# One decoder layer on one core: the small float32 products of two attention heads, and of two state-space groups, made in one visit of TensorE

## The chip, the core and the metric

The kernel runs on one NeuronCore of a Trainium2 chip. The metric is the device time of one execution in microseconds (us), the median of several runs.

## The reference, cut to what matters

The layer normalizes `x` (256 tokens, 2048 channels), multiplies it by one wide input matrix and gives the columns to three branches, whose results are gated, merged, multiplied by an output matrix, added to `x` and normalized again. Two of the branches are touched here.

```python
# stick-breaking attention, 8 heads of 128
logits = einsum('bqhd,bkhd->bhqk', q_blk, k) * scale
log_beta = log_sigmoid(logits)
log_keep = where(earlier, log_beta - logits, 0.0)
later = cumsum(log_keep, axis=3, reverse=True) - log_keep
weights = where(earlier, exp(log_beta + later), 0.0)
out = einsum('bhqk,bkhd->bqhd', weights, v)

# state-space branch, 8 groups of 4 heads, one chunk of 256 tokens
cb = einsum('bclgn,bcsgn->bcgls', cm, bm)
y_diag = einsum('bcgls,bgecls,bcsgep->bclgep', cb, decay_in, xs)
```

The third branch is an attention into 256 memory tokens.

## The kernel before, in words

**The stream of wide products.** Nearly all work is a sequence of matrix products over weights that are read from memory once. A product is cut into chunks. `gemm` (L248) takes chunks of two blocks of 128 input channels by 512 columns, `gemm_cols` (L210) chunks of four such blocks by 256 columns. Each chunk's weights arrive by a DMA of the SP queue in `raw` (four buffers). `split` (L141) then makes two parts of them: ScalarE (ACT) copies `raw` to `wh`, rounded to the fp32r format (L145), and VectorE (DVE) writes the remainder `raw - wh` to `wl` (L149). TensorE (PE) multiplies with both parts in fp32r (L268 to L270 in `gemm`, L228 and L232 in `gemm_cols`). `wh` and `wl` have three buffers each (the pool `stage`, L53), so the `wh` of a chunk can be written only when PE is done with the chunk three places before it. Within a chunk of `gemm_cols` PE first makes two products with `wh` (L228) and then two with `wl` (L232), four times over.

**The order of the other work.** After each chunk the program calls `pump` (L184). It first runs what was put off to this point by `defer` (L171), then one step of one generator. The generators wait in two lanes, and the chunks serve the lanes in turn, so that a generator moves by one step every second chunk. A step issues some instructions and ends at a `yield`. Every engine executes its own instructions in the order in which the program issues them. So the place of an instruction on ACT, between which two chunks' `wh`, is set by the number of `yield`s ahead of it, and nothing is looked up at run time.

**The attention heads.** `sb_head` (L684) is such a generator, and even heads stand in lane 0 and odd ones in lane 1. One head takes these steps: the logits `slg` (L688, L689), two matrix products in plain float32; scale and mask on DVE (L692, L695); `Abs`, `Exp` and `Ln` on ACT, which are the softplus (L698 to L700); a sum and a difference (L702 on DVE, L703 on GpSimd); the split of it (L707); the running sums `scu` in fp32r (L712, L714); a difference (L717); `Exp` on ACT (L719); the value products `spo` in plain float32 (L722, L724); the gating and a split (L728, L731). The heads run while the wide products for the state-space gate `zT` (L746) and then for the convolution channels (L801, `gemm_cols`) stream. The results `oS` are first used by the product with `w_branch_sb` (L984).

**The convolution stage.** Its results are folded (L245 on ACT, L246 on DVE) and go through four taps on DVE (L759 and three of L762), for one half of the columns and, two chunks later, for the other. From the fifth of its eight groups on, the loop at L799 also puts off three `Silu` each, over `zT` and then over the convolution channels (L806, executed in `silu`, L202).

**Function tables.** ACT evaluates `Silu` with another function table than `Exp` and `Ln`. Where the next function is not in the table that is loaded, an `ACT_TABLE_LOAD` stands in ACT's queue ahead of it, put there when the program is compiled. In the state-space part and for the memory heads the program loads a table that holds both `Exp` and `Ln` by hand (L661, L818). In `sb_head` it doesn't.

**The state-space groups.** `ssd_group` (L827) begins with two DMAs on the SP queue and the product `cb` of B and C (L839, L840), in plain float32. `cbs` (L855) is ACT's copy of it. The products `y` (L888) of two neighbouring groups are already made in one step. The eight groups stand in the same lanes behind the heads.

All the small products write to one of four buffers of accumulator memory (`bank`, L87), in turn.

## Time and profile before

| | |
|---|---|
| median of 3 runs | 1207.49 us (1207.31 to 1207.68) |
| the profiled execution's own time | 1207.59 us |
| its span, first instruction to last | 1205.8 us |
| PE busy | 1197.1 us, 99% of the span |
| DVE busy | 802.4 us, 67% |
| ACT busy | 633.8 us, 53% |
| GpSimd (POOL) busy | 49.2 us, 4% |
| granted TensorE clock, mean over the span | 0.998 of full speed |

A row of the profile names the source line, the engine, the operation and the tiles as output<-inputs. A duration runs from an instruction's start on its engine to its end. On PE and ACT the next instruction can start before that end, so that the step from one start to the next is what an instruction costs in a row of them. A float32 product appears as two passes of the same shape, each with a weight load (PEld). "[1.73 <-PE acc L228]" behind a row says that the engine sat idle for 1.73 us before it, until that instruction of PE ended.

### The profile page before, as it was taken

The page shows a single profiled execution, that of the slowest core. Times are in us where ns is not written, and L with a number is a line of the kernel's source. Part 1 is how long each engine was busy: PE and PEld are TensorE (multiplying, and loading weights), DVE is VectorE, ACT ScalarE, POOL GpSimd, SP SyncE. Part 2 cuts the span into 40 slices and gives each one's busy share as a digit, 9 for nine tenths or more (in the row PEclk, how much of TensorE's full clock was granted, in tenths as well). Part 3 has the DMA queues.
Part 4 walks back from the last instruction along what each step waited for, and adds up shares of the span by engine and source line. Part 5 has one row for each costly group of instructions (what it writes and reads, how often), then busy time and mean ns, then how long its engine had stood idle before and what let it go on. Part 6 is the DMA issues. An engine that isn't in the chain of part 4 may idle for free.

```text
span 1205.8 us, 15624 instructions
## 1 busy us (share of the span) xinstructions
PE 1197.1 (99%) x5814; PEld 1005.9 (83%) x5814; DVE 802.4 (67%) x1051; ACT 633.8 (53%) x834; POOL 49.2 (4%) x48
## 2 busy tenths in 40 slices
PE   9999999999999999999999999999999999999997
PEld 8888888888888888888888888888888888888886
DVE  6777664545655555888887858677677655565662
ACT  6665443354355444545655756484757534444551
POOL 0000000000000000010100000000000010110011
PEclk9999999999999999999999999999999999999999
DMA  9677787877765778666668676667766677778952
GB/s 342 224 221 228 226 238 232 250 235 216 211 202 173 208 232 226 185 182 175 175 185 260 209 224 217 210 206 220 226 177 203 206 220 219 228 224 278 301 198 88
DMA packets 168652, 261.52 MB, mean 217 GB/s; under 512 B 11840, under 2 KB 67840, under 8 KB 168448
## 3 DMA queue, kind: packets, MB, share of 16 engines
q1 hardware_dynamic: 134592, 227.94, 63.1%
q10 hardware_dynamic: 33984, 32.59, 8.2%
q8 instruction: 45, 0.74, 0.3%
q14 instruction: 31, 0.25, 0.1%
HBM read 245.78 MB, written 14.71 MB: 216 GB/s over the span
## 4 chain that ended last, share of the span: by engine, by line
PE 98%; issue 1%; DVE 0%; ACT 0%; POOL 0%; POOLq 0%; DVEq 0%; ACTq 0%
PE acc L268 25%; PE acc L270 25%; PE acc L269 25%; PE acc L228 10%; PE acc L232 5%; PE acc L473 4%; PE y L888 1%; PE warm L110 0%; PE dtp L531 0%; PE acc L1089 0%; PE acc L1087 0%; PE acc L1088 0%; PE spo L722 0%; PE slg L688 0%; PE cb L839 0%
## 5 line engine op out<-in xcount | busy, mean ns | idle before, releaser
L149 DVE TENSOR_TENSOR wl<-raw,wh 128x1024 fp32r<-128x1024 f32 (+1 forms) x410 | 504.9, 1233 | 302.6 <-ACT wh L145 296.9
L145 ACT ACTIVATE wh<-raw 128x1024 fp32r<-128x1024 f32 (+1 forms) x410 | 431.9, 1054 | 439.0 <-PE acc L270 339.0
L268 PE MATMUL acc<-wh,hT 128*128 128x512 f32 x896 | 350.9, 392 | 0.0
L270 PE MATMUL acc<-wh,hT 128*128 128x512 f32 x896 | 348.8, 389 | 0.0
L269 PE MATMUL acc<-wl,hT 128*128 128x512 f32 x896 | 348.8, 389 | 0.0
L270 PEld LDWEIGHTS acc<-wh,hT 128*128 128x128 f32 x896 | 168.2, 188 | 35.5
L268 PEld LDWEIGHTS acc<-wh,hT 128*128 128x128 f32 x896 | 168.3, 188 | 34.0 <-issue 0.3
L269 PEld LDWEIGHTS acc<-wl,hT 128*128 128x128 f32 x896 | 168.3, 188 | 33.6
L228 PE MATMUL acc<-hT,wh 128*128 128x512 f32 x512 | 161.5, 397 | 0.0
L232 PEld LDWEIGHTS acc<-hT,wl 128*128 128x128 f32 x512 | 96.2, 188 | 22.7
L232 PE MATMUL acc<-hT,wl 128*128 128x256 f32 x512 | 100.7, 278 | 0.0
L228 PEld LDWEIGHTS acc<-hT,wh 128*128 128x128 f32 x512 | 78.0, 189 | 0.1
L268 PE MATMUL acc<-wh,oD 128*128 128x512 f32 x128 | 49.8, 389 | 0.0
L269 PE MATMUL acc<-wl,oD 128*128 128x512 f32 x128 | 49.8, 389 | 0.0
L270 PE MATMUL acc<-wh,oD 128*128 128x512 f32 x128 | 49.8, 389 | 0.0
L762 DVE SCALAR_TENSOR_TENSOR cT<-cu,wcols,cT 128x255 f32<-128x255 f32 (+2 forms) x96 | 46.4, 483 | 3.4
L969 POOL TENSOR_TENSOR merged<-merged,sig 128x512 f32<-128x512 f32 x16 | 25.8, 1636 | 512.3 <-DVE sig L968 512.3
L268 PE MATMUL acc<-wh,mT 128*128 128x512 f32 x96 | 37.3, 389 | 0.0
L269 PE MATMUL acc<-wl,mT 128*128 128x512 f32 x96 | 37.3, 389 | 0.0
L270 PE MATMUL acc<-wh,mT 128*128 128x512 f32 x96 | 37.3, 389 | 0.0
L473 PE MATMUL acc<-wh,memT 128*128 128x512 f32 x128 | 32.4, 394 | 0.0
L473 PEld LDWEIGHTS acc<-wh,memT 128*128 128x128 f32 x128 | 24.2, 190 | 4.9
(250 smaller groups left out, 1258.6 us busy)
## 6 DMA issues: line engine op xcount, KB each, us to landing
raw<-in_w_in_dram SPq DMA_DIRECT2D x288, 512.0 KB, 4.3
raw<-in_w_branch_ssd_dram SPq DMA_DIRECT2D x32, 512.0 KB, 4.7
raw<-in_w_mem_kv_dram SPq DMA_DIRECT2D x31, 512.0 KB, 5.3
scratch<-blocks ACTq DMA_DIRECT2D x24, 512.0 KB, 4.5
raw<-in_w_out_dram SPq DMA_DIRECT2D x24, 512.0 KB, 6.2
turned<-scratch ACTq DMA_DIRECT2D x64, 128.0 KB, 4.5
raw<-in_w_branch_mem_dram SPq DMA_DIRECT2D x16, 512.0 KB, 4.8
raw<-in_w_branch_sb_dram SPq DMA_DIRECT2D x16, 512.0 KB, 5.0
```

Source lines behind the costliest of these rows:

```text
L145: nc.scalar.activation(hi, src, AF.Copy, **({} if scale is None else {"scale": scale}))
L149: nc.vector.tensor_tensor(lo, src, h32, ALU.subtract)
L228: nc.tensor.matmul(halves[b], wh[:, kt - k0, b * P:(b + 1) * P], lhs.both(kt), start=first, stop=False, skip_group_check=True)
L232: nc.tensor.matmul(halves[b][:, 1], wl[:, kt - k0, b * P:(b + 1) * P], lhs.at(kt)[0], start=False, stop=last, skip_group_check=True)
L268: nc.tensor.matmul(a, lh[:, tt], wh[:, j], start=first, stop=False)
L269: nc.tensor.matmul(a, lh[:, tt], wl[:, j], start=False, stop=False)
L270: nc.tensor.matmul(a, ll[:, tt], wh[:, j], start=False, stop=last)
L473: nc.tensor.matmul(acc[g][:, t], a[:, t * P:(t + 1) * P], w[:, g], start=(k == 0 and i in (0, 3)), stop=(k == NKT - 1 and i > 3))
L762: nc.vector.scalar_tensor_tensor(a[:, s:T], u[:, 0:T - s], convw[:, 3 - s, i:i + 1], a[:, s:T], ALU.mult, ALU.add)
L888: nc.tensor.matmul(y[c:c + 64, b, t * P:(t + 1) * P], xs[:, s, 64 * e:64 * e + 64], dec[j][:, e], start=(j == 0), stop=(j == 2), skip_grou ...
L969: nc.gpsimd.tensor_tensor(merged[t][:, cs], merged[t][:, cs], sig[:, t], ALU.add)
```

## The change

Three pairs of products are brought together. The even head's first step makes the `slg` of both heads of a pair, and the odd head's first step makes nothing. The `spo` of an even head is put off to the step of the odd head one chunk later, where both heads' products are issued in one go; each head has one more `yield` behind it. In the state-space part the even group's first step makes the `cb` of both groups.

```diff
@@ -681,13 +681,23 @@
     ra = const.tile([P, P], F32R, name="ra")
     rb = const.tile([P, P], F32R, name="rb")
 
+    logits = {}
+    weighed = []
+
+    def products(bank, left, right):
+
+        nc.tensor.matmul(bank[:, 0:3:2], left[:, 0:P], right, start=True, stop=True)
+        nc.tensor.matmul(bank[:, 1], left[:, P:T], right[:, P:T], start=True, stop=True)
+
     def sb_head(h):
         hs = slice(h * P, (h + 1) * P)
 
-        lg = bank([P, 3, P], "slg")
-        nc.tensor.matmul(lg[:, 0:3:2], kS[:, h, 0:P], qS[:, h], start=True, stop=True)
-        nc.tensor.matmul(lg[:, 1], kS[:, h, P:T], qS[:, h, P:T], start=True, stop=True)
-        yield
+        if h not in logits:
+            for i in (h, h ^ 1):
+                logits[i] = bank([P, 3, P], "slg")
+                products(logits[i], kS[:, i], qS[:, i])
+        yield
+        lg = logits[h]
         lm = ta([P, 3, P], "lm")
         nc.vector.scalar_tensor_tensor(lm[:, 0:2], lg[:, 0:2], 128.0 ** -0.5,
                                        smask.unsqueeze(1).to_broadcast([P, 2, P]),
@@ -719,11 +729,20 @@
         nc.scalar.activation(lm, lm, AF.Exp)
         yield
         po = bank([P, T], "spo")
-        nc.tensor.matmul(po, vS[:, 0, hs], lm[:, 0:3:2], start=True, stop=False,
-                         skip_group_check=True)
-        nc.tensor.matmul(po[:, P:T], vS[:, 1, hs], lm[:, 1], start=False, stop=True,
-                         skip_group_check=True)
-        yield
+
+        def weigh():
+            nc.tensor.matmul(po, vS[:, 0, hs], lm[:, 0:3:2], start=True, stop=False,
+                             skip_group_check=True)
+            nc.tensor.matmul(po[:, P:T], vS[:, 1, hs], lm[:, 1], start=False, stop=True,
+                             skip_group_check=True)
+
+        weighed.append(weigh)
+        if len(weighed) == 2:
+            while weighed:
+                weighed.pop(0)()
+        yield
+        yield
+        assert weigh not in weighed
         o = tq([P, T], "so")
         nc.vector.tensor_tensor(o.rearrange("p (i c) -> p i c", c=32),
                                 po.rearrange("p (i c) -> p i c", c=32),
@@ -811,6 +830,7 @@
     oD = []
     ssd_done = []
     pair = []
+    scores = {}
 
     def exp_ln():
 
@@ -834,10 +854,15 @@
         h0 = heads[0]
         for j in range(2):
             nc.sync.dma_start(dec[j], acT[j, h0:h0 + 4].partition_broadcast(P))
-        cb = bank([P, 3, P], "cb")
         bT, cTT = cT[2], cT[3]
-        nc.tensor.matmul(cb[:, 0:2], bT[:, g, 0:P], cTT[:, g], start=True, stop=True)
-        nc.tensor.matmul(cb[:, 2], bT[:, g, P:T], cTT[:, g, P:T], start=True, stop=True)
+        if g not in scores:
+            for i in (g, g ^ 1):
+                scores[i] = bank([P, 3, P], "cb")
+                nc.tensor.matmul(scores[i][:, 0:2], bT[:, i, 0:P], cTT[:, i], start=True,
+                                 stop=True)
+                nc.tensor.matmul(scores[i][:, 2], bT[:, i, P:T], cTT[:, i, P:T], start=True,
+                                 stop=True)
+        cb = scores[g]
         yield
         xs = tb([P, 2, T], "xs")
         rows = x_rows[g // 2]
```

The instruction rows of DVE, GpSimd, SP and PE are the same in number before and after (953 on DVE, for one); ACT has 864 rows before and 870 after.

On PE, at the first pair of heads, before the change (`acc` is the wide product for `zT`, `slg` the logits of head 0):

```order
L270 MATMUL acc_3082<-wh_3121,hT_127 128x512
L688 MATMUL slg_3142<-qS_1932,kS_1933 128x2x128
L689 MATMUL slg_3142<-qS_1932,kS_1933 128x128
L268 MATMUL acc_3082<-wh_3147,hT_127 128x512
L269 MATMUL acc_3082<-wl_3148,hT_127 128x512
L270 MATMUL acc_3082<-wh_3147,hT_127 128x512
```

and after it:

```order
L270 MATMUL acc_3082<-wh_3121,hT_127 128x512
L689 MATMUL slg_3142<-qS_1932,kS_1933 128x2x128
L690 MATMUL slg_3142<-qS_1932,kS_1933 128x128
L689 MATMUL slg_3145<-qS_1932,kS_1933 128x2x128
L690 MATMUL slg_3145<-qS_1932,kS_1933 128x128
L268 MATMUL acc_3082<-wh_3150,hT_127 128x512
L269 MATMUL acc_3082<-wl_3151,hT_127 128x512
```

The logits of head 1 (`slg_3145`) moved from one chunk later to directly behind those of head 0.

On ACT, in the convolution stage, at the `Abs`, `Exp` and `Ln` of heads 6 and 7 before the change (`wh` is the weight split of a chunk, `sp` the softplus of a head, L698 to L700; no table load stands among them):

```order
L145 ACTIVATE wh_4737<-raw_4735 128x1024
L698 ACTIVATE sp_4761<-lm_4704 128x384
L699 ACTIVATE sp_4761<-sp_4761 128x384
L700 ACTIVATE sp_4761<-sp_4761,ones 128x384
L145 ACTIVATE wh_4767<-raw_4765 128x1024
L698 ACTIVATE sp_4787<-lm_4732 128x384
L699 ACTIVATE sp_4787<-sp_4787 128x384
L700 ACTIVATE sp_4787<-sp_4787,ones 128x384
L145 ACTIVATE wh_4794<-raw_4792 128x1024
```

and six chunks later, at the first `Silu` over `zT` and up to the `Exp` of L719 (`lm`, head 6):

```order
L145 ACTIVATE wh_4906<-raw_4904 128x1024
L202 ACT_TABLE_LOAD
L202 ACTIVATE zT_3079<-zT_3079 128x1024
L145 ACTIVATE wh_4938<-raw_4936 128x1024
L245 ACTIVATE cu_4958<-acc_4791 128x512
L202 ACTIVATE zT_3079<-zT_3079 128x1024
L145 ACTIVATE wh_4969<-raw_4967 128x1024
L202 ACTIVATE zT_3080<-zT_3080 128x1024
L145 ACTIVATE wh_4997<-raw_4995 128x1024
L145 ACTIVATE wh_5021<-raw_5019 128x1024
```

After the change, the steps of heads 6 and 7 stand six chunks later, since three pairs of heads ahead of them each took one step of two chunks more. `Abs`, `Exp` and `Ln` are now L708 to L710. First head 6, behind the `wh` of the chunk at the same place as `wh_4906` above:

```order
L145 ACTIVATE wh_4886<-raw_4884 128x1024
L202 ACT_TABLE_LOAD
L202 ACTIVATE zT_3079<-zT_3079 128x1024
L708 ACTIVATE sp_4911<-lm_4855 128x384
L709 ACT_TABLE_LOAD
L709 ACTIVATE sp_4911<-sp_4911 128x384
L710 ACT_TABLE_LOAD
L710 ACTIVATE sp_4911<-sp_4911,ones 128x384
L145 ACTIVATE wh_4917<-raw_4915 128x1024
L245 ACTIVATE cu_4937<-acc_4771 128x512
L202 ACT_TABLE_LOAD
L202 ACTIVATE zT_3079<-zT_3079 128x1024
```

and directly behind these rows head 7, to the end of the third `Silu`:

```order
L708 ACTIVATE sp_4941<-lm_4880 128x384
L709 ACT_TABLE_LOAD
L709 ACTIVATE sp_4941<-sp_4941 128x384
L710 ACT_TABLE_LOAD
L710 ACTIVATE sp_4941<-sp_4941,ones 128x384
L145 ACTIVATE wh_4947<-raw_4945 128x1024
L202 ACT_TABLE_LOAD
L202 ACTIVATE zT_3080<-zT_3080 128x1024
L145 ACTIVATE wh_4976<-raw_4974 128x1024
L145 ACTIVATE wh_5001<-raw_4999 128x1024
```

The three `Silu` of this place (`zT`) stand between the same chunks as before; the `Abs`, `Exp` and `Ln` came between them, with a table load ahead of each `Exp` and each `Ln`, and a load ahead of each `Silu`. The six rows more on ACT are table loads: in the whole kernel there are 20 before and 26 after.

## The prediction

> **What bounds the kernel now.** The page comes first: how busy the engines are, and the chain of work that ended last.

> ```profile
> PE 1197.1 (99%) x5814; PEld 1005.9 (83%) x5814; DVE 802.4 (67%) x1051; ACT 633.8 (53%) x834; POOL 49.2 (4%) x48
> PE 98%; issue 1%; DVE 0%; ACT 0%; POOL 0%; POOLq 0%; DVEq 0%; ACTq 0%
> ```

> Then the waits of PE, all of them:

> ```profile
> PE warm L110 <- POOL ones L99: 1.1, 1, 1.1
> ```

> PE is never late once the stream runs. So the time falls only by what PE's own stream loses, and it rises by any wait that PE is given. I ask both: what is a visit's edge worth, and does any other engine fall behind far enough to be noticed?

> **The edges of the visits.** The timeline of PE at the logits of head 0, with ordinary products before and behind (start, length, engine, line):

> ```profile
> 380.83 0.39 PE L268 MATMUL acc<-wh,hT 128*128 128x512 f32 x1
> ...
> 382.65 0.39 PE L270 MATMUL acc<-wh,hT 128*128 128x512 f32 x1
> 382.88 0.59 PE L688 MATMUL slg<-qS,kS 128*128 128x256 f32 x2
> 383.31 0.38 PE L689 MATMUL slg<-qS,kS 128*128 128x128 f32 x2
> 383.44 0.47 PE L268 MATMUL acc<-wh,hT 128*128 128x512 f32 x1
> 383.76 0.39 PE L269 MATMUL acc<-wl,hT 128*128 128x512 f32 x1
> ```

> From 380.83 to 382.65 lie eight steps of the stream, 0.2275 us each. From 382.65 to 383.76 lie two such steps and the visit: 1.11 - 0.455 = 0.655 us. The visit's own passes: two of 256 columns take 383.31 - 382.88 = 0.43, and two of 128, half as wide, 0.215 more; together 0.645. The edge is the rest, 0.01 us, and with these rounded starts between 0 and 0.03. The change drops 12 visits (four each of `slg`, `spo` and `cb`): **-0.12 us**, at most -0.36.

> **The heads that arrive later.** A head has one step more, so each later pair starts two chunks later than the pair ahead of it did: heads 6 and 7 come six chunks later. That moves their `Abs`, `Exp` and `Ln` into the chunks in which the first three `Silu` stand, with seven table loads in place of one. The timeline of ACT shows both pieces as they are now, first the heads alone, then the `Silu`:

> ```profile
> 563.44 0.60 ACT L245 ACTIVATE cu<-acc 128x512 f32<-128x512 f32 x1 [2.61 <-PE acc L232]
> 563.93 1.05 ACT L145 ACTIVATE wh<-raw 128x1024 fp32r<-128x1024 f32 x1
> 564.88 0.52 ACT L698 ACTIVATE sp<-lm 128x384 f32<-128x384 f32 x1
> 565.43 0.53 ACT L699 ACTIVATE sp<-sp 128x384 f32<-128x384 f32 x1
> 565.99 0.62 ACT L700 ACTIVATE sp<-sp,ones 128x384 f32<-128x384 f32 x1
> ...
> 580.63 1.06 ACT L145 ACTIVATE wh<-raw 128x1024 fp32r<-128x1024 f32 x1 [1.31 <-issue]
> 581.71 1.28 ACT L202 ACT_TABLE_LOAD   x1
> 583.00 1.06 ACT L202 ACTIVATE zT<-zT 128x1024 f32<-128x1024 f32 x1
> 583.97 1.04 ACT L145 ACTIVATE wh<-raw 128x1024 fp32r<-128x1024 f32 x1
> ```

> From start to start that gives: `cu` 0.49, `wh` 0.95 (1.08 ahead of a load, which waits for its end), `Abs` 0.55, `Exp` 0.56, `Ln` about 0.6, a load 1.29, `Silu` 0.97.

> How far is ACT ahead? First the group of all `wh` (count, busy time and mean; idle time before them, and what ended it), then PE at a chunk's start in the same stage:

> ```profile
> L145 ACT ACTIVATE wh<-raw 128x1024 fp32r<-128x1024 f32 (+1 forms) x410 | 431.9, 1054 | 439.0 <-PE acc L270 339.0 <-PE acc L228 39.2 <-issue 21.4
> ```

> ```profile
> 580.61 0.63 PE L228 MATMUL acc<-hT,wh 128*128 128x512 f32 x2
> 581.08 0.39 PE L232 MATMUL acc<-hT,wl 128*128 128x256 f32 x2
> ...
> 586.18 0.63 PE L228 MATMUL acc<-hT,wh 128*128 128x512 f32 x2
> ```

> Between the first and the last of these rows lie eight rounds of L228 and L232, which are two chunks: a chunk takes 2.79 us, and its first products with `wl` follow 0.47 after its start. `wh` has three buffers, and ACT mostly waits for PE to free one (L228 is its product with `wh` in this stage), so the `wh` at 580.63 is that of the chunk which PE begins at 586.18. ACT's lead is two chunks, 5.57 us, less 1.06 for the `wh` itself: it may spend 4.5 us more before PE notices, and each further chunk gives it 2.79.

> Now the queue, by the order of the changed kernel. Zero is 580.61; call the chunks A (`wh_4886`), B (`wh_4917`), C (`wh_4947`), D (`wh_4976`) and E. PE wants A at 5.57, B at 8.36, C at 11.15, D at 13.94, E at 16.72.

> - ACT writes A's `wh` from 0.02; load 1.10, `Silu` 2.39, `Abs` 3.36, load 3.91, `Exp` 5.20, load 5.76, `Ln` 7.05, B's `wh` 7.65, done **8.70**.
> - `cu` 8.60, load 9.22, `Silu` 10.51, `Abs` 11.48, load 12.03, `Exp` 13.32, load 13.88, `Ln` 15.17, C's `wh` 15.77, done **16.82**.
> - Load 16.85, `Silu` 18.14, D's `wh` 19.11, done 20.16. From here ACT is ahead again.

> DVE makes each `wl` after its `wh`, and it has other work in its queue; its timeline now:

> ```profile
> 576.48 0.55 DVE L702 SCALAR_TENSOR_TENSOR sp<-lm,sp 128x384 f32<-128x384 f32 x1
> ...
> 578.08 1.11 DVE L759 TENSOR_SCALAR cT<-cu,wcols 128x256 f32<-128x256 f32 x1
> ...
> 583.88 0.41 DVE L759 TENSOR_SCALAR cT<-cu,wcols 128x256 f32<-128x256 f32 x1
> 584.32 1.52 DVE L762 SCALAR_TENSOR_TENSOR cT<-cu,wcols,cT 128x255 f32<-128x255 f32 x3
> 585.76 1.22 DVE L149 TENSOR_TENSOR wl<-raw,wh 128x1024 fp32r<-128x1024 f32 x1
> ```

> PE then meets these waits.

> - B: begins at 8.73 instead of 8.36, waits 0.34. Its `wl` ends at 8.73 + 1.22 = 9.95, PE wants it at 9.17: 0.78. B ends at 9.95 + 2.32 = 12.27.
> - C: begins at 16.82, waits **4.55** (592.9 to 597.4 of the old clock). `wl` again 0.78 late; C ends at 20.39.
> - D: its `wh` is there. But behind C's `wl` (18.07) DVE first makes four taps (1.9) and a head's `sp` (0.55), so D's `wl` runs from 20.5 to 21.72, and PE wants it at 20.86: 0.86. D ends at 24.04.
> - E: `wl` at 23.5, in time. E begins at 24.04, not 16.72.

> Sum 0.34 + 0.78 + 4.55 + 0.78 + 0.86 = **7.31 us**, all on the path, since PE has no other idle time to give back.

> The bounds: some 16 steps of ACT at 0.05 each, 0.8 either way. Beyond E, DVE is 0.4 early for its next `wl`; if the first tap takes 1.11, as at 578.08, and not 0.41, another 0.3 is lost. So 6.5 to 8.4, and I take 7.3.

> [...]

> **Edits with one answer.** The `cb` of two groups, and the two `spo`, are ready on PE a chunk before or after their old place, and no row of PE's waits names them. The pairs take four buffers in turn as before, and each claim falls on one whose reader ran many chunks earlier. The heads end eight chunks later, and what follows them is far off (first and last start in us behind the colon):

> ```profile
> L145 ACT ACTIVATE oS<-so x8: 417/418/418, 430.3 to 612.2; 128x256 fp32r<-128x256 f32 x8
> ```

> ```profile
> L839 PE MATMUL cb<-cT,cT x16: 377/377/378, 666.5 to 864.3; 128*128 128x256 f32 x16
> ```

> The last `oS` at 612.2 moves by 8 x 2.79 + 7.3 to about 642. The first of the groups, which stand behind the heads in the same lanes, comes at 666, and the product with `oS` later still: hidden, with 24 us to spare. SP's queue keeps its order; `raw` only waits longer.

> **The rivals.**

> *The clock drops in the gap.* PE would stand still for 4.55 us. The end of the kernel shows what that can do: the last product, and two windows behind it (each engine's busy time, then the granted clock, here 0.94 and 0.50).

> ```profile
> 1197.91 0.28 PE L1089 MATMUL acc<-wlh,mT 128*128 128x256 f32 x1
> ```

> ```profile
> 1200.00:1202.00 2.00, 0.00 (x0) 0.00 (x0) 1.14 (x3) 0.94 (x1) 0.14 (x1) 0.94 0.24 87
> 1202.00:1205.80 3.80, 0.00 (x0) 0.00 (x0) 0.00 (x0) 0.00 (x0) 0.00 (x0) 0.50 0.59 230
> ```

> And the timeline of PE at the kernel's start:

> ```profile
> 1.06 5.06 PE L110 MATMUL warm<-ones 128*128 128x128 f32 x22 [1.06 <-POOL ones L99]
> ...
> 7.39 1.55 PE L473 MATMUL acc<-wh,memT 128*128 128x512 f32 x6
> ```

> 0.94 as a mean of 1.00 and 0.50 puts the fall at 1202 - 0.12 x 2 = 1201.76, 3.6 us after the last product ended at 1198.19. At the start, passes of 128 columns come 0.22 us apart until 6.1, twice the 0.107 of the visit above, and from 7.39 the stream is at full speed (1.55 for six): the clock took about 6 us to rise. One fall after 3.6 us and one rise after 6 are all that the trace has. A gap of 4.55 lies 0.4 of the way between them, so I give the drop a little less than even odds. [...] The price: at half speed for 6 us from 16.82, C's products end at 22.7 instead of 20.39 (its wait for `wl` shrinks to 0.3), D's at 25.6 instead of 24.04, with no wait: +1.6. That gives 7.3 + 1.6 - 0.1 = 8.8, **1216.3 us**.

> *Not slower: the lead hides it.* This decides if the loads are much shorter than 1.29 when the table changes twice in a row. C's `wh` would have to be done at 11.15, not 16.82; six loads lie ahead of it, so each would have to take 0.35 us or less. The load at 581.71 takes 1.28, and nothing in the rows makes a second one shorter. Then only the edges remain, 1207.49 - 0.12 = **1207.4 us**.

> [...]

> **How the numbers follow.** The sum for the profiled execution is 1207.59 + 7.31 - 0.12 = 1214.8; the median of the runs lies 0.10 lower, so **1214.7 us**. Chances: the waits without the drop 0.53 (1213.9 to 1215.8 by the bounds), with the drop 0.35 (1215.5 to 1217.4), hidden 0.06, the emptied engine 0.04, and 0.02 for a gain that no row prices. The range 1213.5 to 1217.4 holds the first two, 0.88, less what the bounds may miss. Slower by over 0.2% (2.4 us, about what a measurement of this kernel can tell) is 0.92, no change 0.06, faster 0.02.

> **What would show it.** In the profile after: table loads in L709 and L710, two each, and five in L202, of 1.28 us; a wait of PE for ACT's `wh` of about 4.5 us near 593, and three for DVE's `wl` of 0.8 around it; no other wait. Visits of `slg` in pairs of about 1.3 us. The granted clock between 597 and 604 tells the first rival. If PE shows no wait there, or if one stands in another place (a head's `scu`, a `cb`), the working is wrong.

## The result and the profile after

The changed kernel takes **1215.88 us** (median of 5 runs, 1215.34 to 1216.09) against 1207.49 (1207.31 to 1207.68): a ratio of 1.0069, 95% interval 1.0057 to 1.0080, 8.4 us slower. The forecast was 1214.7 in a range of 1213.5 to 1217.4. The profiled execution took 1215.89 us.

The page after: its span, how busy the engines are, and the chain that ended last.

```profile
span 1214.2 us, 15632 instructions
PE 1200.8 (99%) x5814; PEld 1007.6 (83%) x5814; DVE 803.0 (66%) x1051; ACT 641.1 (53%) x840; POOL 49.1 (4%) x48
PE 97%; ACT 1%; issue 1%; DVE 0%; POOL 0%; POOLq 0%; DVEq 0%; ACTq 0%
```

ACT is busy for 7.3 us more, about what six table loads of 1.28 us add, and it now stands in the chain with 1% (0% before). The waits of PE:

```profile
PE acc L228 <- ACT wh L145: 4.1, 1, 4.1
PE warm L110 <- POOL ones L99: 1.1, 1, 1.1
PE acc L232 <- DVE wl L149: 0.5, 1, 0.5
```

One long wait for ACT and one for DVE are new. Three waits for `wl` were forecast; PE shows one of 0.5, and its weight loads (PEld) two, 1.7 us in all. ACT's timeline at the place of the prediction's queue (A's `wh` at 580.34, B's at 587.86, C's at 595.84):

```profile
580.34 1.06 ACT L145 ACTIVATE wh<-raw 128x1024 fp32r<-128x1024 f32 x1 [3.04 <-PE acc L228]
581.42 1.28 ACT L202 ACT_TABLE_LOAD   x1
...
584.21 1.28 ACT L709 ACT_TABLE_LOAD   x1
585.50 0.53 ACT L709 ACTIVATE sp<-sp 128x384 f32<-128x384 f32 x1
586.04 1.28 ACT L710 ACT_TABLE_LOAD   x1
...
587.86 1.04 ACT L145 ACTIVATE wh<-raw 128x1024 fp32r<-128x1024 f32 x1
...
595.84 1.04 ACT L145 ACTIVATE wh<-raw 128x1024 fp32r<-128x1024 f32 x1
596.89 1.28 ACT L202 ACT_TABLE_LOAD   x1
```

From A's `wh` B's is 7.52 us away (7.63 in the working) and C's 15.50 (15.75). Around a load ACT has no idle time to speak of: the load starts 0.01 to 0.03 us behind the end of the row ahead of it, and `Exp` 0.01 us behind the load. PE's timeline around its stop:

```profile
588.96 0.73 PE L228 MATMUL acc<-hT,wh 128*128 128x512 f32 x2
590.22 0.51 PE L232 MATMUL acc<-hT,wl 128*128 128x256 f32 x2 [0.53 <-DVE wl L149]
...
592.42 0.39 PE L232 MATMUL acc<-hT,wl 128*128 128x256 f32 x2
596.93 1.22 PE L228 MATMUL acc<-hT,wh 128*128 128x512 f32 x2 [4.12 <-ACT wh L145]
598.19 0.80 PE L232 MATMUL acc<-hT,wl 128*128 128x256 f32 x2
598.78 1.05 PE L228 MATMUL acc<-hT,wh 128*128 128x512 f32 x2
```

Behind the stop a pair of products takes 1.05, not 0.63. The granted clock (third number from the end) says why:

```profile
589.70:593.00 3.30, 2.59 (x14) 2.13 (x14) 1.06 (x2) 3.27 (x4) 0.00 (x0) 1.00 0.49 140
593.10:596.40 3.30, 0.00 (x0) 0.00 (x0) 0.00 (x0) 3.26 (x5) 0.00 (x0) 1.00 0.03 10
596.50:603.20 6.70, 6.23 (x18) 4.84 (x19) 6.18 (x9) 5.74 (x7) 1.96 (x2) 0.50 0.31 86
603.30:612.00 8.70, 8.70 (x52) 7.60 (x52) 8.49 (x14) 4.01 (x6) 1.60 (x1) 1.00 0.61 182
```

The clock fell to half for 6.8 us. So the first rival came in, the wait with the drop. And the visits, at the logits of the first pair:

```profile
382.36 0.39 PE L270 MATMUL acc<-wh,hT 128*128 128x512 f32 x1
382.59 0.59 PE L689 MATMUL slg<-qS,kS 128*128 128x256 f32 x2
...
383.24 0.60 PE L689 MATMUL slg<-qS,kS 128*128 128x256 f32 x2
...
384.13 0.40 PE L269 MATMUL acc<-wl,hT 128*128 128x512 f32 x1
```

Of 384.13 - 382.36 = 1.77 us, two steps of the stream are 0.455; the pair costs 1.315, twice the 0.655 of one visit. The pairing saves nothing there. For `spo` the chunk steps say the same: in the kernel before, two visits lengthen them by 0.58, 0.65 and 0.08 us, and here a pair by 1.23 and 0.09.

To compare the experiments, here is by how much each chunk's step exceeded 2.79 us, in us, read from the starts of the products with `wh` in PE's timelines (chunks A to F, F being the one behind E; none of these steps holds a visit):

```
                      A     B     C     D     E     F     sum
worked out, no drop  0.34  5.33  0.78  0.86  0     0-0.3  7.31
changed kernel       0.23  5.18  2.91  0.31  0     0      8.63
e3_joint_table       0     3.14  2.02  0     0     0.61   5.77
e4_fill_gap          0.22  5.19  0.91  0.69  0     1.04   8.05
e5_four_buffers      0     2.77  2.47  0     0     0.19   5.43
e6_silu_later        0     0     0     0     0     0.49   0.49
e8_dve_subtract      0.22  5.19  0.91  1.28  0     0.10   7.70
```

The changed kernel's 8.63 less 0.28 is the difference of the spans, 8.4: its trace was already 0.28 ahead at the first convolution product (466.79 against 467.07). Its clock rose earlier at the kernel's start (5.96 against 7.09), but that this is the cause isn't shown: in experiment 3 it rose at 4.81, and that product came at 467.14.

### The profile page after: what moved, and what is told of

Its sections match the earlier page's. It is cut to its first block, busy times and chain, and to the rows that moved or that the text cites. A ratio compares the mean times of both kernels' runs of the same rounds, so it can differ in the third digit from the quotient of the medians.

```text
span 1214.2 us, 15632 instructions
## 1 busy us (share of the span) xinstructions
PE 1200.8 (99%) x5814; PEld 1007.6 (83%) x5814; DVE 803.0 (66%) x1051; ACT 641.1 (53%) x840; POOL 49.1 (4%) x48
## 4 chain that ended last, share of the span: by engine, by line
PE 97%; ACT 1%; issue 1%; DVE 0%; POOL 0%; POOLq 0%; DVEq 0%; ACTq 0%
PE acc L268 25%; PE acc L269 25%; PE acc L270 25%; PE acc L228 9%; PE acc L232 5%; PE acc L473 4%; PE y L913 1%; PE warm L110 0%; PE dtp L531 0%; PE acc L1114 0%; PE acc L1112 0%; PE acc L1113 0%; PE spo L734 0%; PE cb L861 0%; PE slg L689 0%
## 5 line engine op out<-in xcount | busy, mean ns | idle before, releaser
L149 DVE TENSOR_TENSOR wl<-raw,wh 128x1024 fp32r<-128x1024 f32 (+1 forms) x410 | 505.0, 1233 | 316.3 <-ACT wh L145 310.0
L145 ACT ACTIVATE wh<-raw 128x1024 fp32r<-128x1024 f32 (+1 forms) x410 | 431.6, 1054 | 445.7 <-PE acc L270 340.1
L268 PE MATMUL acc<-wh,hT 128*128 128x512 f32 x896 | 350.4, 391 | 0.0
L270 PE MATMUL acc<-wh,hT 128*128 128x512 f32 x896 | 348.8, 389 | 0.0
L269 PE MATMUL acc<-wl,hT 128*128 128x512 f32 x896 | 348.8, 389 | 0.0
L270 PEld LDWEIGHTS acc<-wh,hT 128*128 128x128 f32 x896 | 168.2, 188 | 35.3
L268 PEld LDWEIGHTS acc<-wh,hT 128*128 128x128 f32 x896 | 168.2, 188 | 34.3 <-issue 0.3
L269 PEld LDWEIGHTS acc<-wl,hT 128*128 128x128 f32 x896 | 168.3, 188 | 33.8
L228 PE MATMUL acc<-hT,wh 128*128 128x512 f32 x512 | 163.5, 401 | 4.2 <-ACT wh L145 4.1
L232 PEld LDWEIGHTS acc<-hT,wl 128*128 128x128 f32 x512 | 97.2, 190 | 24.7 <-DVE wl L149 1.7
L232 PE MATMUL acc<-hT,wl 128*128 128x256 f32 x512 | 101.9, 281 | 0.6 <-DVE wl L149 0.5
L228 PEld LDWEIGHTS acc<-hT,wh 128*128 128x128 f32 x512 | 79.2, 191 | 4.7 <-ACT wh L145 4.6
L268 PE MATMUL acc<-wh,oD 128*128 128x512 f32 x128 | 49.8, 389 | 0.0
L269 PE MATMUL acc<-wl,oD 128*128 128x512 f32 x128 | 49.8, 389 | 0.0
L270 PE MATMUL acc<-wh,oD 128*128 128x512 f32 x128 | 49.8, 389 | 0.0
L268 PE MATMUL acc<-wh,mT 128*128 128x512 f32 x96 | 37.3, 389 | 0.0
L269 PE MATMUL acc<-wl,mT 128*128 128x512 f32 x96 | 37.3, 389 | 0.0
L270 PE MATMUL acc<-wh,mT 128*128 128x512 f32 x96 | 37.3, 389 | 0.0
L473 PE MATMUL acc<-wh,memT 128*128 128x512 f32 x128 | 32.0, 390 | 0.0
L713 POOL TENSOR_TENSOR lm<-lm,sp 128x384 f32<-128x384 f32 x8 | 11.4, 1428 | 417.2 <-DVE sp L712 416.4
```

Source lines behind the costliest of these rows:

```text
L145: nc.scalar.activation(hi, src, AF.Copy, **({} if scale is None else {"scale": scale}))
L149: nc.vector.tensor_tensor(lo, src, h32, ALU.subtract)
L228: nc.tensor.matmul(halves[b], wh[:, kt - k0, b * P:(b + 1) * P], lhs.both(kt), start=first, stop=False, skip_group_check=True)
L232: nc.tensor.matmul(halves[b][:, 1], wl[:, kt - k0, b * P:(b + 1) * P], lhs.at(kt)[0], start=False, stop=last, skip_group_check=True)
L268: nc.tensor.matmul(a, lh[:, tt], wh[:, j], start=first, stop=False)
L269: nc.tensor.matmul(a, lh[:, tt], wl[:, j], start=False, stop=False)
```

## The experiments

The theory: ACT's queue, with the table loads of the late heads among the `Silu`, starves PE, and the clock's fall comes on top. The rivals: the pairing itself costs; the fall is most of it; the late heads cost by something else than the loads.

**1. The pairing without the later heads** (from the changed kernel).

```diff
         yield
-        yield
         assert weigh not in weighed
```

> All three pairings are kept, but the second yield behind a head's value products is taken out again, so that heads 6 and 7 reach their Abs, Exp and Ln where they did before the change; ACT has 20 table loads, as before. If the loss comes from ACT's queue (table loads of the late heads among the Silu), PE has no wait in the convolution stage and the time is that of the kernel before, 1207.5 us within 0.4; a pair of visits costs 1.36 us, twice one visit, so nothing is gained by the pairing. If the pairing itself costs (long visits, two accumulator banks claimed at once), the time stays near 1215.9.

Measured: 1208.71 us against 1207.41, ratio 1.0011 (1.0002 to 1.0020). Some 7 of the 8.4 us are gone, and with them the long visits as their cause. (A pair costs 1.315 us by the rows above, not the 1.36 of the expectation.) But 1.3 us are left, outside what I expected. For the instructions on `spo`, what their engines sat idle for and who waited (us, times), and then the waits of PE's weight loads:

```profile
  PE spo L736: 10.5, 4
  DVE so L746: 10.5, 4
```

```profile
PEld acc L232 <- DVE wl L149: 1.9, 4, 0.5
```

Without the second step DVE reaches the gating `so` of a pair's first head one chunk after PE was given its value products, while DVE runs about two chunks ahead of PE (in the kernel before, the `wl` that DVE begins at 486.06 is multiplied from 492.34 on: two chunks of 2.79 us and the visits between them). It stands in its queue for 10.5 us in four waits (1.3 in two in the kernel before, by the same view), and four times a `wl` behind it is late for PE. Four chunk steps are longer for it, by 0.35, 0.35, 0.35 and 0.22 us, 1.27 in all.

**2. The later heads without the pairing** (from the kernel before).

```diff
         yield
+        yield
         o = tq([P, T], "so")
```

> The kernel before with nothing but one more yield behind each head's value products: no pairing at all. Queue theory: the heads come six chunks late, 26 table loads, the same waits as with the whole change, 1215 to 1216.2 us. If the pairing itself costs: 1207.5.

Measured: 1215.32 us against 1207.41, ratio 1.0066 (1.0054 to 1.0079). The step alone makes 7.9 of the 8.4 us, and the two intervals overlap, so that no rest can be told from noise.

**3. Two loads fewer at the crowded place.**

```diff
         sp = t4([P, 3, P], "sp")
+        if h > 5:
+            nc.scalar.preload_act_table_set("natural_log_exp_and_others")
         nc.scalar.activation(sp, lm, AF.Abs)
```

> The whole change, but heads 6 and 7 load by hand the table that holds Exp and Ln both: two loads fewer (24) at the crowded place. Queue theory, by the steps of the prediction: B's weights are ready at 7.45 and in time, C's at 14.35 instead of 16.82, so PE waits 3.2 for C, 0.8 for its remainder and 0.9 in D: 4.9 in all, and the gap is too short for the clock to fall: 1212.3 us (1211.5 to 1213). If the clock's fall is most of the loss: about 1209. If the number of loads does not matter: 1215.9.

Measured: 1213.26 us against 1207.41, ratio 1.0049 (1.0037 to 1.0062). The wait for C came as worked out (3.14 for 3.2; B was in time), so the time does follow the number of loads: C's `wh` starts 13.23 us behind A's, not 15.50, 1.1 us for each load. (The total fell by 2.6, but a shorter fall of the clock is part of that.) The rest was wrong: I had said that the gap is too short for the clock to fall.

```profile
588.50:591.80 3.30, 3.30 (x21) 2.78 (x19) 1.48 (x2) 3.25 (x4) 0.00 (x0) 1.00 0.36 99
591.90:595.30 3.40, 0.45 (x3) 0.29 (x2) 0.31 (x1) 3.31 (x6) 0.00 (x0) 1.00 0.14 47
595.40:598.70 3.30, 3.02 (x10) 2.14 (x9) 3.19 (x7) 3.29 (x4) 0.00 (x0) 0.50 0.38 101
598.80:602.20 3.40, 3.40 (x21) 2.95 (x21) 3.40 (x4) 1.90 (x3) 2.82 (x2) 1.00 0.50 152
```

It fell, for 3.4 us, and chunk C lost 2.02 in place of 0.78. The total is 1.0 above the expectation.

**4. The gap filled with work.**

```diff
         nc.scalar.activation(sp, sp, AF.Ln, bias=ones[:, 0:1])
+        if h == 6:
+            fill = bank([P, P], "fill")
+            for _ in range(16):
+                nc.tensor.matmul(fill, ones, ones, start=True, stop=True)
         yield
```

> The whole change, and 16 more float32 products of the constant ones (3.4 us, their result is read by nobody) on PE between chunks B and C, where PE stands still for 4.1 us. ACT's queue is untouched. Queue theory: the waits stay, only the clock does not fall: 1.4 us less than the changed kernel, 1214.4 us (1214.0 to 1215.0). If the clock's fall is most of the loss: 1209 to 1210. If it costs nothing: 1215.9.

Measured: 1215.36 us against 1207.41, ratio 1.0066 (1.0053 to 1.0080). The clock stayed up (1.00 in each window from 589.8 to 603.4, a mean of 0.999), and C's step is 0.91 over, not 2.91. But only 0.5 us of the total came back, not 1.4, since in chunk F PE is late again by 1.04. DVE's timeline there, and GpSimd's:

```profile
600.36 1.22 DVE L149 TENSOR_TENSOR wl<-raw,wh 128x1024 fp32r<-128x1024 f32 x1
601.49 1.38 DVE L716 SCALAR_TENSOR_TENSOR sp<-lm,sp 128x384 f32<-128x384 f32 x1
602.80 1.21 DVE L149 TENSOR_TENSOR wl<-raw,wh 128x1024 fp32r<-128x1024 f32 x1
603.93 1.10 DVE L782 TENSOR_SCALAR cT<-cu,wcols 128x256 f32<-128x256 f32 x1
```

```profile
600.61 1.84 POOL L717 TENSOR_TENSOR lm<-lm,sp 128x384 f32<-128x384 f32 x1 [70.28 <-PE acc L228]
603.04 1.84 POOL L717 TENSOR_TENSOR lm<-lm,sp 128x384 f32<-128x384 f32 x1 [0.59 <-DVE sp L716]
```

The burst leaves DVE with work in arrears, and beside GpSimd two of its instructions take 1.38 and 1.10 where they took 0.55 and 0.41. The changed kernel has the same two (1.36 and 1.10), and F's step isn't longer there (0 over in the table): while the clock is down, at 0.50, PE falls behind and finds its `wl` ready; with the clock up, at 1.00, it waits, and the step is 1.04 over. One of the changed kernel's five runs had the clock of the kernel before (a mean of 0.998 where the other four show 0.996) and took 1215.34 us, what this experiment gives.

**5. A longer lead for ACT**: four buffers of `wh` in the three places where it is claimed; one of them:

```diff
-            wh = stage.tile([P, KCC, 2 * P], F32R, tag="wh", name=nm("wh"))
+            wh = stage.tile([P, KCC, 2 * P], F32R, tag="wh", name=nm("wh"), bufs=4)
```

> The whole change, and four buffers of wh in place of three, so that ACT may run one chunk (2.79 us) further ahead of PE; wl keeps three. Queue theory: B is in time, C's weights are ready 2.8 earlier, so PE waits 2.9 for them, 0.8 for C's remainder and 0.9 in D: 4.5 in all, with a gap too short for the clock to fall: 1212.0 us (1211.3 to 1212.8). If ACT is not ahead by the third chunk (the raw weights land too late), nothing is gained: 1215.9.

Measured: 1213.12 us against 1207.36, ratio 1.0048 (1.0036 to 1.0061). B is in time, and C's wait is 2.77 for the 2.9 expected: here the buffer was worth about a chunk of lead, since A's and B's steps together fell from 5.41 to 2.77 over, by 2.64 us, where a chunk is 2.79. The total is 1.1 above the expectation, and again the clock fell, behind a window with 0.73 us of work:

```profile
592.20:595.50 3.30, 0.73 (x2) 0.30 (x2) 1.22 (x2) 3.27 (x4) 0.00 (x0) 1.00 0.00 0
595.60:599.00 3.40, 3.40 (x11) 3.02 (x12) 3.29 (x7) 3.40 (x5) 0.97 (x1) 0.50 0.51 154
```

**6. The late heads, with the `Silu` out of their way.**

```diff
-                silu(waiting.pop(0), 6 if not waiting else 1 + j)
+                silu(waiting.pop(0), 6 if not waiting else (7 if i == 4 else 1) + j)
```

> The whole change, late heads included, but the first three Silu are put off by six chunks more, so that they stand behind the Exp and Ln of heads 6 and 7; 20 table loads. Queue theory: no wait of PE, 1207.5 us within 0.4. If the later heads cost by something else than the loads (DVE, the buffers, the accumulator banks), the time stays above 1212.

Measured: 1207.83 us against 1207.36, ratio 1.0004 (0.9995 to 1.0013). The loads of `L202` are three again, and PE has one wait left, for DVE at chunk F.

```profile
L202 ACT ACT_TABLE_LOAD x3 | 3.8, 1283 | 0.1
```

```profile
PEld acc L232 <- DVE wl L149: 0.7, 1, 0.7
```

So late heads as such cost half a microsecond. The rest is the crowd on ACT, loads and `Silu` together: this edit takes both away. That the loads alone carry much of it is shown by experiment 3.

**7. The pairing with neither cost**: experiment 1, with the gating put off by two chunks, so that it doesn't hold up the head's lane.

```diff
         assert weigh not in weighed
-        o = tq([P, T], "so")
...
+
+        def gate():
+            o = tq([P, T], "so")
...
+        defer(gate, 2)
         yield
```

> All three pairings, no extra yield (20 table loads), and the gating of a head's result (so, oS) put off by two chunks without holding up its lane, so that DVE does not reach it before PE has made the value products. If e1_no_extra_step lost its 1.3 us to DVE waiting for spo (10.5 us in four waits, and PE then four times 0.35 late for wl), this kernel has neither that nor the table loads: 1207.4 us within 0.4, no faster than the kernel before, since a pair costs PE twice a visit. If the pairs cost something by themselves, it stays near 1208.7; if they gain, it is under 1206.8.

Measured: 1207.39 us against 1207.29, ratio 1.0001 (0.9992 to 1.0010). In its trace the 24 chunks that begin with the one two places before A take 69.41 us (580.38 to 649.79), and in the kernel before 69.40 (580.61 to 650.01). PE has no wait for another engine behind the start:

```profile
PE warm L110 <- POOL ones L99: 1.1, 1, 1.1
```

All pairs are in place here, and the time is that of the kernel before. This was also the candidate for a kernel better than both; it isn't one.

**8. GpSimd's part in DVE's arrears** (from experiment 4).

```diff
-        nc.gpsimd.tensor_tensor(lm, lm, sp, ALU.subtract)
+        (nc.vector if h > 5 else nc.gpsimd).tensor_tensor(lm, lm, sp, ALU.subtract)
```

> e4_fill_gap with the difference lm - sp of heads 6 and 7 on DVE in place of GpSimd. There the two GpSimd differences (1.84 us each) run beside a DVE instruction that took 1.38 in place of 0.55 and one that took 1.10 in place of 0.41, 1.5 us in all, and PE is late for wl twice more, 0.6 and 0.9. If the engines slow each other, DVE saves 1.5 and pays two differences of 0.5: about 0.5 us less than e4_fill_gap, 1214.9. If not, DVE has 1.0 more to do and the time is 1216 or more.

Measured: 1214.96 us against 1207.29, ratio 1.0064 (1.0051 to 1.0077): 0.3 to 0.4 below experiment 4 (0.28 by the differences from the kernel before, 0.35 by the table), though DVE has two instructions more. The totals alone hardly tell that from noise; the rows do. The step of F falls from 1.04 to 0.10, and D's rises from 0.69 to 1.28. Where GpSimd is silent, the same two instructions take their old time:

```profile
602.10 0.55 DVE L716 SCALAR_TENSOR_TENSOR sp<-lm,sp 128x384 f32<-128x384 f32 x1
602.68 0.56 DVE L717 TENSOR_TENSOR lm<-lm,sp 128x384 f32<-128x384 f32 x1
603.16 1.22 DVE L149 TENSOR_TENSOR wl<-raw,wh 128x1024 fp32r<-128x1024 f32 x1
604.29 0.41 DVE L782 TENSOR_SCALAR cT<-cu,wcols 128x256 f32<-128x256 f32 x1
```

A further variant of experiment 4, with neither engine making the two differences, gave no time.

## Why the prediction was right, and where it was off

- **The cause: right.** The step alone makes the loss, as far as can be told (2), the pairs alone make none (7), and with the `Silu` moved away all but 0.5 us of it goes (6). The time goes down with two loads fewer (3) and with a longer lead (5), both through the wait for C's `wh`, as the queue was worked out.
- **The queue's terms: right in size.** A's step 0.23 for 0.34, and B's, which holds the late `wl` and the wait for C, 5.18 for 5.33. ACT's steps between A's and C's `wh` were together 0.25 us shorter than I took them.
- **The emptied engine** (given 0.04): no run shows a switch of tables that empties ACT first, or that costs much beyond the load's own row. Each load took 1.28 us, the rows beside it stand 0.01 to 0.03 us away, before the change and after it, and the row ahead only lost its overlap with the next: in the changed kernel a `wh` takes 1.08 us from start to start ahead of a load (580.34 to 581.42) and 0.95 otherwise (587.86 to 588.81).
- **The likeliest case was the wrong one of two.** I gave 0.53 to a clock that stays and 0.35 to one that falls. It fell in the profile and, by their mean clocks, in four of five runs. Of the working, the step that failed is the reading of "one fall after 3.6 us and one rise after 6" as a delay into which a gap falls more or less far: the falls of experiments 3 and 5 came with gaps of 3.0 and 2.6 us. By the bounds found in the last section, an estimate, the forecast gap of 4.55 us would always have brought the fall: wherever it lies on the grid, one step has at most 3.41 - 4.55/2 = 1.14 us of work left. The measured gap of 4.12 leaves at most 1.35, between the bounds.
- **The price of the fall was mis-sized**: +1.6 forecast, +0.4 to 0.6 measured (1215.88 against 1215.36, each less its kernel before, and 8.63 against 8.05 in the table). It isn't one number: experiment 2, where the mean clock shows the fall in all five runs, took 1215.14 to 1216.03. The sum for a clock that stays was too low by 0.7 (1214.7 for 1215.36): "beyond E" I allowed 0.3 for DVE's backlog, and it was 1.04. Both errors have one root. DVE sets the pace behind the burst (in the changed kernel it is busy for 6.18 of the 6.70 us from 596.5 and for 8.49 of the 8.70 from 603.3), so PE's slower clock hides under DVE's arrears. The two errors cancelled in part, and that the rival's sum, 1216.3, came within 0.4 of the result is in part luck.
- **The edges: nothing, where -0.12 was forecast.** A pair of `slg` takes 1.315 us and a visit 0.655, and the chunks with `spo` agree; for `cb` only the total of experiment 7 speaks. By these numbers what stands above the passes' own time comes with each visit's passes, not with the change between products; the numbers of the rounded starts did not forbid zero. Why it is so was not tried.
- **The first head of a pair** is the odd one, not the even one as described before: the products that experiment 4 issues in head 6's step stand behind chunk B on PE, where the second head's softplus is. No sum depends on it.
- What was not looked for: taking the step out is not free either. It gave DVE time; without it DVE waits for PE (1).

## What to carry to other kernels

A `yield` or a stage more in one generator moves everything behind it on every engine, and its price is decided by what it comes to stand beside. Before such a change, read in the new instruction order where functions of different tables now alternate on ACT, add up that queue between two pieces of work that the busiest engine needs, and compare it with the lead that the buffers give. And when the busiest engine has stopped once, ask which engine is in arrears afterwards: here it was DVE that, beside the clock, set the pace of the recovery (with the clock up, in experiment 4, F's step was still 1.04 over).

## What the runs showed of the hardware

```profile
1198.33:1201.74 3.41, 1.24 (x11) 1.04 (x9) 1.11 (x4) 0.70 (x3) 0.67 (x1) 1.00 0.00 0
1201.74:1205.10 3.36, 0.00 (x0) 0.00 (x0) 0.95 (x3) 0.74 (x1) 0.00 (x0) 0.50 0.68 262
```

```profile
1196.69:1200.10 3.41, 1.63 (x14) 1.42 (x12) 0.92 (x3) 0.51 (x2) 0.51 (x1) 1.00 0.00 0
1200.10:1203.51 3.41, 0.00 (x0) 0.00 (x0) 1.14 (x3) 0.94 (x1) 0.16 (x1) 1.00 0.57 223
```

  The step ahead of a fall was not always an idle one: over a third of it was work in experiment 1 (1.24 of 3.41). So a gap of 2.6 us was enough, by its place on the grid: in experiment 5 some 2.1 us of it, and a second stop of 0.53, lay in one step.
- **A fall behind a stop lasted one step or two.** One (3.4 us) in experiments 3 and 5, where PE worked 3.1 and 3.4 us of it; two (6.8 us) in the changed kernel and in experiment 2, where PE had worked 2.9 us of the first.
- **DVE beside GpSimd.** In experiment 4 the DVE instruction that starts at 601.49 ends at 602.87, 0.42 us behind the end of GpSimd's (602.45), and the one at 603.93 ends 0.15 behind GpSimd's second (604.88). The two `wl`, which start 0.25 us ahead of GpSimd's instructions, keep their length (1.22 and 1.21). So beside GpSimd these two instructions took 0.83 and 0.69 us more than with GpSimd silent (0.55 and 0.41 in experiment 8). That DVE stands still to the end of GpSimd's instruction isn't shown: 0.42 and 0.15 are less than the usual 0.55 and 0.41. What lengthens them and not the `wl` was not tried.
